# Loading the GLU's gate weights ahead of its value weights, and giving the transposes of the gated product a PSUM bank of their own

## The chip, the core and the metric

The kernel runs on one core of a Trainium2 chip. The metric is the device time of one execution in microseconds (us); three runs of the kernel before were timed and their median counts. Engines are named as in the profile: PE (TensorE matmuls), PEld (TensorE weight loads, which overlap with PE), DVE (VectorE), ACT (ScalarE), POOL (GpSimd) and SP (SyncE, which issues most DMAs). One execution is also profiled, and every number from a trace belongs to that execution.

## The reference: what is computed

One layer of a hybrid encoder on a sequence of 2048 tokens, model width 1024, all in float32. The input is normed and projected into six groups of 512 columns. One group goes through a state-space model, a GELU and a GLU; three more are q, k and v of an 8-head stick-breaking attention; the last two gate these results. Both are joined, projected by W_out and added to the input. Last comes a gated product: a second norm, a projection by W_pg, a sigmoid, and a product with a second, smaller projection of another input p.

```
proj = rmsnorm(x) @ w_in                    # u, g_ssm, q, k, v, g_attn
z    = gelu(S5(u))
val, gate = split(z @ w_glu + b_glu)        # the GLU: w_glu is 512 x 1024
y_ssm = val * sigmoid(gate) * silu(g_ssm)
y_att = stick_breaking(q, k, v) * silu(g_attn)
h    = x + concat(y_ssm, y_att) @ w_out     # the mixed product
out  = h + sigmoid(rmsnorm(h) @ w_pg) * (p @ w_pp)   # the gated product
```

## The kernel before

The work goes through four stages. The first (to about 120 us) projects and prepares the state-space inputs. The second runs the state-space model in eight batches, with the first gate projections. The third is the attention: four passes, each for a pair of heads, over 16 blocks of 128 queries; the passes are staggered by SKEW = 8 steps, so that there are 40 steps (L1215) in which up to two passes are active. In the last ten steps, from glu_at = 30 on, the GLU runs beside the last passes. The fourth stage is phase_out (L1032): eight "mixed" pairs (L945) of 128-token blocks through W_out, then eight "gated" pairs (L988) through W_pg. Both use a seven-product scheme for a 2 x 2 block matrix product (cross_products, L903).

**Precision.** Every float32 operand is split into a rounded part "hi" and a remainder "lo" (split, L511: an ACT copy, then a DVE subtraction), and each product takes three matmuls (mm3, mm3x).

**Weights.** load_w (L473) loads a weight matrix in blocks of 128 x 512 (256 KB). For each block it takes a tile of the ring "w" (16 buffers), a staging buffer "wst" (two buffers at that time), issues the DMA on SP (L486), and splits the block into the tile: ACT copy (L513 by way of L488), DVE subtraction. The DMA of a block can't start until a staging buffer is free, and the copy can't start until the tile's earlier contents are no longer needed.

**GLU.** glu_load (L666) loads the two halves of w_glu, each of four blocks: half 0 makes "val", half 1 makes "gate". It is called once, at the end of step glu_at - 1 (L1243), and loads half 0, then half 1. Of the eight tiles that it takes in the ring, the first four were last used by pass 1 of the attention, the other four by pass 2, whose last projection is in step glu_at - 1. glu_z (L671) loads and splits z: four DMAs "zt" per 512 tokens. glu_unit (L684) computes one 128 x 512 piece of the output: the gate's twelve matmuls into bank "ssm" (tile ps_g2, shown as ps_g in the profile), the value's twelve into bank "acc" (ps_v), then ACT sigmoid, DVE, POOL, and a DMA.

**PSUM.** There are eight banks, named by tags: z0, z1, tr, acc, ssm, o, and w0, w1. bank(name, *tags) (L1120) deals out the given tags in turn for each name. Until step 29 the attention's projections use acc, ssm and tr in turn, later acc and tr only (L44), which leaves ssm to the GLU's gate.

**Gated product.** gated_pair (L988) works on a pair of 128-token blocks, as four tiles h[0] to h[3] of 128 x 512. Each tile is loaded (L995, ring "h" of seven buffers), transposed by four PE transposes into one bank (ps_t, L997 to L999), and copied by ACT to a "yq" tile (L1001, ring of five). cross_products then makes sums and differences of these (POOL, tag "sx", L912), splits them, and runs seven products of twelve matmuls into four accumulators ps[0] to ps[3] (L921): six tags in turn. early and late (L1009, L1014) take the accumulators out: late(k) adds on DVE, takes a sigmoid on ACT (L1020), computes the second weight's product p @ w_pp of six matmuls into ps_p (L1021), multiplies on DVE (L1025), adds h (L1026), and stores. The second weight's product needs nothing but its weights, p and a bank, so it may run early. ps_t and ps_p both take "tr" and "o" in turn.

**Order.** The order of the instructions on each engine isn't the program's. A planner (arrange, L1554; list_schedule, L1446) collects all instructions with their dependencies and durations of its own estimate, simulates the engines forward and backward six times, and keeps the order with the shortest simulated end. Each engine then executes in that order and waits where its next instruction isn't ready. A tile of a tag is opened in the order of the program. The planner picks the most urgent of the instructions that it takes to be ready, and if there is one only, that one.

Of the kernel before, what the change touches and what calls it, by code (L numbers as in the profile page):

```python
# [74 lines left out]
def stt(nc, out, a, s, b, op0, op1):  # L75
    nc.vector.scalar_tensor_tensor(out, a, s, b, op0=op0, op1=op1)  # L76
# [396 lines left out]
def load_w(e, blocks, width, scale, tag="w", pool=None, bufs=None, at=0, act=True, spare=None):  # L473

    nc = e.nc
    out = []
    for c, src in enumerate(blocks, at):
        t = (pool or e.wpool).tile([P, 2, width], F32R, tag=tag, name=f"w_{tag}", **({"bufs": bufs} if bufs else {}))
        hi, lo = t[:, 0], t[:, 1]
        if spare is None or c < STB + STA:  # L480
            raw = e.stage[c % len(e.stage)].tile([P, 512], F32, tag="wst", name="wst")[:, :width]
        else:
            raw = spare.tile([P, L, NCH // 2], F32, tag="uq", name="wst", bufs=4).rearrange("p j c -> p (j c)")[:, :width]
        if c == MARK0 and spare is not None:
            e.mark(0)
        e.wdma(raw.rearrange("p (k c) -> p k c", k=src.shape[1]) if len(src.shape) == 3 and src.shape[0] == P else raw, src)  # L486
        if scale is None:
            split(e, hi, lo, raw)  # L488
        else:
            if act:  # L490
                nc.scalar.activation(hi, raw, AF.Copy, scale=scale[:, c:c + 1])  # L491
            else:
                vs(nc, hi, raw, scale[:, c:c + 1], ALU.mult)
            stt(nc, lo, raw, scale[:, c:c + 1], hi.bitcast(F32), ALU.mult, ALU.subtract)
        out.append(t)
    return out
# [14 lines left out]
def split(e, hi, lo, src):  # L511

    e.nc.scalar.activation(hi, src, AF.Copy)  # L513
    vt(e.nc, lo, src, hi.bitcast(F32), ALU.subtract)
# [148 lines left out]
    return xt  # L663


def glu_load(e):  # L666
    rows = e.w_glu[0].rearrange("(g h) n -> h g n", h=GH)
    return [load_w(e, [rows[4 * c:4 * c + 4, :, 512 * k:512 * k + 512] for c in range(4)], 512, None) for k in range(2)]


def glu_z(e, pool, tb):  # L671
# [231 lines left out]
def cross_products(e, pool, name, q, w, early, late, eng=None):  # L903

    nc = e.nc

    def f(tag, n):
        return pool.tile([P, 512], F32, tag=tag, name=tag, bufs=n)

    def add(a, b, op=ALU.add):  # L910
        t = f("sx", 3)
        (eng or nc.gpsimd).tensor_tensor(t, a, b, op=op)  # L912
        return t

    def product(ps, a, k, first):
        y = pool.tile([P, 2, 4, P], F32R, tag="yr", name="yr", bufs=4)
        split(e, y[:, 0].rearrange("p c t -> p (c t)"), y[:, 1].rearrange("p c t -> p (c t)"), a)
        for c in range(4):
            mm3x(e, ps, (y[:, 0, c], y[:, 1, c]), (w[k][c][:, 0], w[k][c][:, 1]), first and c == 0, c == 3, not first)

    ps = [e.bank(name, "z0", "z1", "acc", "ssm", "w0", "w1") for _ in range(4)]  # L921
    product(ps[0], q[0], 0, True)
    s1 = add(q[2], q[3])
    s2 = add(s1, q[0], ALU.subtract)
    r = f("r", 1)
    nc.scalar.activation(r, ps[0], AF.Copy)
    product(ps[1], s2, 1, True)
    u = f("u", 2)
    vt(nc, u, ps[1], r, ALU.add)
    product(ps[2], s1, 2, True)  # L930
    early(u, ps[2], 0)
    s3 = add(q[0], q[2], ALU.subtract)
    product(ps[3], s3, 3, True)
    early(u, ps[3], 1)
    product(ps[0], q[1], 4, False)
    late(0, ps[0], None)
    late(3, None, None)
    s4 = add(q[1], s2, ALU.subtract)
    product(ps[2], s4, 5, False)
    late(1, ps[2], u)  # L940
    product(ps[3], q[3], 6, False)
    late(2, ps[3], u)
# [45 lines left out]
def gated_pair(e, pool, far, j, rs):  # L988

    nc = e.nc  # L990
    q, h = [], []
    for k in range(4):
        i, m = k // 2, k % 2
        t = far.tile([P, 512], F32, tag="h", name="h", bufs=7)
        nc.sync.dma_start(t, e.h_d[2 * j + i][:, 512 * m:512 * m + 512])  # L995
        h.append(t)
        ps = e.bank("ps_t", "tr", "o")  # L997
        for c in range(4):
            nc.tensor.transpose(ps[:, c * P:(c + 1) * P], t[:, c * P:(c + 1) * P], e.ident)  # L999
        y = pool.tile([P, 512], F32, tag="yq", name="yq", bufs=5)  # L1000
        nc.scalar.activation(y, ps, AF.Copy)  # L1001
        q.append(y)
    pt = far.tile([P, 2, 256], F32, tag="pt", name="pt", bufs=1)
    nc.sync.dma_start(pt, e.p[0, 0].rearrange("(c p) t -> p c t", p=P)[:, :, 256 * j:256 * j + 256])
    pr = far.tile([P, 2, 2, 256], F32R, tag="pr", name="pr", bufs=1)
    split(e, pr[:, 0].rearrange("p c t -> p (c t)"), pr[:, 1].rearrange("p c t -> p (c t)"), pt.rearrange("p c t -> p (c t)"))
    o = [None] * 4

    def early(u, ps, n):  # L1009
        if n == 0:  # L1010
            o[3] = far.tile([P, 512], F32, tag="sg", name="sg", bufs=4)
        vt(nc, o[3], ps, o[3] if n else u, ALU.add)

    def late(k, ps, u):  # L1014
        i, m = k // 2, k % 2
        if o[k] is None:
            o[k] = far.tile([P, 512], F32, tag="sg", name="sg", bufs=4)
            if u is not None:
                vt(nc, o[k], ps, u, ALU.add)
        nc.scalar.activation(o[k], ps if k == 0 else o[k], AF.Sigmoid, scale=rs[:, i:i + 1])  # L1020
        pp = e.bank("ps_p", "tr", "o")  # L1021
        ts = slice(i * P, i * P + P)
        for c in range(2):
            mm3x(e, pp, (pr[:, 0, c, ts], pr[:, 1, c, ts]), (e.wp[m][c][:, 0], e.wp[m][c][:, 1]), c == 0, c == 1)
        vt(nc, o[k], pp, o[k], ALU.mult)  # L1025
        (nc.vector if j == NT // 2 - 1 else nc.gpsimd).tensor_tensor(o[k], o[k], h[k], op=ALU.add)  # L1026
        nc.sync.dma_start(e.out[0, (2 * j + i) * P:(2 * j + i + 1) * P, 512 * m:512 * m + 512], o[k])

    cross_products(e, pool, "ps_g", q, e.wg, early, late)


# [13 lines left out]
def hybrid_block_kernel(ctx: ExitStack, tc: tile.TileContext, x, xt, small, p, w_in, ssm_w_glu, w_out, w_ple_gate,  # L1045
                        w_ple_proj, out, rows, pools, dbg=None):
    nc = tc.nc
    e = Env()
# [59 lines left out]
    def pool(stack, name, bufs=1, space=None, side=None):  # L1108
        kw = {} if space is None else {"space": space}
        if side:  # L1110
            kw["side"] = side
        pools.append(stack.enter_context(tc.tile_pool(name=name, bufs=bufs, reuse_waits="tile", **kw)))
        return pools[-1]
# [58 lines left out]
    with e.later():  # L1172
        wgate = load_w(e, row_blocks(e.w_in[0], NC8, 512), 512, e.gmix)
# [19 lines left out]
    t = 0  # L1193
# [27 lines left out]
    glu_at = steps - 10  # L1221
    for t in range(steps):
        e.z_banks, e.q_banks, e.o_banks = BANKS[2 if t < SKEW - 2 else t >= glu_at]
        for hp in range(NHP):
            if 0 <= t - SKEW * hp < NT:
                attn_block(e, ap, A[hp], t - SKEW * hp)
        if t == glu_at:
            over.close()
            gl = pool(over, "glu")
        for hp in range(NHP):  # L1230
            i = t - SKEW * hp
            if 0 <= i + 2 < NT and i + 2 >= (AHEAD if hp == 0 else 0):
                attn_proj(e, ap1, A[hp], i + 2, xg[:, i % 2] if hp == 0 and i < AHEAD else None)
            if i == -WE and hp:
                attn_w(e, A[hp], 0, 4, **(dict(pool=wx, bufs=4) if hp == 2 else {}))
            if i == -3 and hp:
                attn_w(e, A[hp], 4, NC8)
        if t == AHEAD - 1:
            left.close()
            e.xp = pool(ctx, "xp")  # L1240
            kv2 = pool(left, "kv2")
            wx = pool(over, "wx")
        if t == glu_at - 1:  # L1243
            wglu = glu_load(e)
        if t >= glu_at:
            for k in glu_units[t - glu_at]:
                if k % 4 == 0:
                    zr = glu_z(e, gl, k // 4)
                glu_unit(e, old, (6, 7) if t >= glu_at + 2 else (6,), wglu, zr, k // 4, k % 4)
            c = t - glu_at - 2  # L1250
            if c >= 0:
                cross_sums(e, old, *((w_out[0], e.so_d, None) if c < 4 else (w_ple_gate[0], e.sg_d, e.gple)), c % 4)
        if t == steps - 3:
            e.wo = [cross_weights(e, e.w_out[0], e.so_d, None, p) for p in range(2)]
            wo4 = cross_weights(e, e.w_out[0], e.so_d, None, 4, pool=Halves(e))
# [358 lines left out]
```

## Time and profile before

| | |
|---|---|
| timed runs | 1490.81, 1491.39, 1494.24 us; median 1491.39 |
| the profiled execution's own time | 1490.92 us |
| its span in the trace | 1489.2 us |
| its mean granted TensorE clock | 0.995 |
| first GLU gate matmul, first GLU value matmul | 863.6 us, 879.4 us after the span's start |
| transposes of the gated product (128 of them) | from 1254.8 to 1459.1 us |
| last second-weight matmul | 1484.1 us |

In lines of the timeline and of the groups, the columns are: start, duration (or count), engine, line of the kernel, operation, output <- inputs, shapes; in brackets the idle time of the engine just before and what ended it. Lines of waits give who waited, for whom, the total in us, how many times, and the longest. Lines of windows give the stretch, its length, the busy time of each engine with its instructions, the granted clock of PE (1.00 is full speed), and the DMA engines' share and rate. L65, L76 and L513 are lines of helpers that serve many places, so there the tile names tell which one is meant.

### The profile page before, as it was taken

To read this page: it belongs to the slowest core of one execution; us is meant where nothing else is said; L and a number is where in the kernel's file an instruction comes from. 1 tells how busy PE (TensorE), PEld (TensorE's weight loads), DVE (VectorE), ACT (ScalarE), POOL (GpSimd) and SP (SyncE) were. 2 spreads that over 40 slices of the span, in tenths; PEclk is the share of its full clock that TensorE was granted. 3 is DMA by queue.
4 is the path that set the end of the run, shared out by engine and by line. 5 is a ranking of instruction groups with operands and counts; after the bars stand their busy time and mean duration, and the time that the engine had idled before them with its cause. 6 is when DMAs were issued, how large, how long until landed. Compare 5 with 4: busy or idle time off the path is not lost.

```text
span 1489.2 us, 33570 instructions
## 1 busy us (share of the span) xinstructions
PE 1444.9 (97%) x13068; PEld 1220.6 (82%) x13068; DVE 1012.0 (68%) x1814; ACT 812.1 (55%) x1764; POOL 469.2 (32%) x512
## 2 busy tenths in 40 slices
PE   5999999999999999999999999999999999999998
PEld 5999989988888888887788877787777888777776
DVE  8943877976567876777766766657777557744544
ACT  5654545565456765566655655566654436533333
POOL 3221354412221111211122114544234555434332
PEclk9999999999999999999999999999999999999999
DMA  8876746645332523334333445766477546423221
GB/s 292 296 267 231 227 135 206 194 152 169 126 131 99 180 99 101 126 120 141 97 125 126 125 131 183 234 223 187 131 243 243 170 156 196 151 76 107 72 67 60
DMA packets 178909, 238.21 MB, mean 160 GB/s; under 512 B 65744, under 2 KB 121024, under 8 KB 167616
## 3 DMA queue, kind: packets, MB, share of 16 engines
q1 hardware_dynamic: 176368, 227.49, 47.2%
q0 software_dynamic: 2384, 8.59, 2.0%
q8 instruction: 103, 1.69, 0.5%
q14 instruction: 54, 0.44, 0.1%
HBM read 166.94 MB, written 64.90 MB: 156 GB/s over the span
## 4 chain that ended last, share of the span: by engine, by line
PE 77%; DVE 9%; DMA 4%; issue 4%; ACT 3%; POOL 2%; SPq 1%; DVEq 0%; POOLq 0%; ACTq 0%
PE ps_q L745 20%; PE ps_o L843 7%; PE ps_z L812 6%; PE ps_wt L526 4%; PE ps_g L707 4%; PE ps_g L709 4%; PE ps_g L708 3%; PE ps_h L709 3%; PE ps_h L707 3%; PE ps_h L708 3%; DMA wst<-in_ssm_w_glu_dram 2%; PE ps_u L541 1%; PE ps_u L543 1%; PE ps_u L542 1%; PE ps_sg L541 1%
## 5 line engine op out<-in xcount | busy, mean ns | idle before, releaser
L821 DVE TENSOR_TENSOR_SCAN px<-px,ps_z 128x512 f32<-128x512 f32 (+3 forms) x320 | 339.4, 1085 | 102.6 <-ACT px L816 64.5
L745 PE MATMUL ps_q<-w_w,xt 64*128 64x512 f32 x2784 | 372.5, 398 | 1.6 <-DVE old L76 0.9
L745 PEld LDWEIGHTS ps_q<-w_w,xt 64*128 64x128 f32 x2784 | 269.1, 185 | 41.1 <-DVE old L76 1.5
L816 ACT ACTIVATE px<-ps_z 128x512 f32<-128x512 f32 (+3 forms) x320 | 159.5, 534 | 82.5 <-PE ps_z L812 80.8
L835 ACT ACTIVATE ws<-ps_wt 128x512 f32<-128x512 f32 (+3 forms) x320 | 160.3, 537 | 71.8 <-PE ps_wt L526 67.4
L812 PE MATMUL ps_z<-k,q 64*128 64x512 f32 (+3 forms) x960 | 138.0, 381 | 2.1 <-DVE px L821 1.1
L843 PE MATMUL ps_o<-ws,v 128*64 128x128 f32 x2176 | 136.9, 278 | 0.0
L843 PEld LDWEIGHTS ps_o<-ws,v 128*64 128x64 f32 x2176 | 118.6, 138 | 17.0 <-issue 13.7
L507 POOL TENSOR_TENSOR rs_qk<-rs_qk,mhalf 128x4 f32<-128x4 f32 x64 | 67.2, 1050 | 186.5 <-DVE rs_qk L72 183.9
L526 PEld LDWEIGHTS ps_wt<-ident,px 64*128 64x128 f32 x2176 | 94.5, 139 | 29.1 <-ACT ws L835 8.0
L526 PE MATMUL ps_wt<-ident,px 64*128 64x64 f32 x2176 | 100.5, 224 | 5.7 <-ACT ws L835 5.0
L812 PEld LDWEIGHTS ps_z<-k,q 64*128 64x128 f32 x960 | 86.9, 186 | 21.8 <-issue 5.4
L819 POOL TENSOR_SCALAR_AFFINE_SELECT px<-px 128x128 f32<-128x128 f32 x128 | 40.5, 326 | 175.7 <-ACT px L816 167.5
L756 POOL TENSOR_TENSOR v<-qn,v 128x128 f32<-128x128 f32 x64 | 30.9, 483 | 167.6 <-DMA v<-qn 147.8
L541 PE MATMUL ps_u<-xt,w_w 128*128 128x256 f32 x256 | 74.3, 292 | 8.1 <-ACT w_w L491 6.8
L543 PE MATMUL ps_u<-xt,w_w 128*128 128x256 f32 x256 | 73.2, 292 | 2.9 <-DVE w_w L76 2.9
L542 PE MATMUL ps_u<-xt,w_w 128*128 128x256 f32 x256 | 73.8, 289 | 0.5 <-DVE xt L65 0.5
L1026 POOL TENSOR_TENSOR sg<-sg,h 128x512 f32<-128x512 f32 x28 | 39.3, 1412 | 99.7 <-DVE sg L65 90.7
L65 DVE TENSOR_TENSOR yr<-sx,yr 128x512 fp32r<-128x512 f32 x64 | 49.2, 790 | 31.1 <-ACT yr L513 30.2
L65 DVE TENSOR_TENSOR qn<-ps_q,part 128x512 f32<-128x512 f32 x54 | 36.8, 682 | 44.2 <-ACT part L751 40.9
L513 ACT ACTIVATE yr<-sx 128x512 fp32r<-128x512 f32 x64 | 39.3, 629 | 50.2 <-POOL sx L912 17.6
L541 PEld LDWEIGHTS ps_u<-xt,w_w 128*128 128x128 f32 x256 | 50.3, 197 | 8.9 <-ACT w_w L491 7.0
(438 smaller groups left out, 3464.0 us busy)
## 6 DMA issues: line engine op xcount, KB each, us to landing
xt<-hn SPq DMA_DIRECT2D x58, 1024.0 KB
hn<-xt SPq DMA_DIRECT2D x16, 1024.0 KB
h<-h SPq DMA_DIRECT2D x64, 256.0 KB
wst<-in_w_in_dram SPq DMA_DIRECT2D x48, 256.0 KB
xg<-hn SPq DMA_DIRECT2D x12, 1024.0 KB
out_dram<-sg SPq DMA_DIRECT2D x32, 256.0 KB
x<-in_x_dram SPq DMA_DIRECT2D x14, 512.0 KB
h<-in_x_dram SPq DMA_DIRECT2D x28, 256.0 KB
```

The costliest lines, as they stand in the source:

```text
L526: e.nc.tensor.transpose(ps[h][:, 64 * k:64 * k + 64], v[r], e.ident[r, r])
L541: mm(out, wh, xh, start=first, stop=False)
L542: mm(out, wh, xl, start=False, stop=False)
L707: mm(out, xh, wh, start=first, stop=False, skip_group_check=more)
L708: mm(out, xh, wl, start=False, stop=False, skip_group_check=more)
L709: mm(out, xl, wh, start=False, stop=last, skip_group_check=more)
L745: nc.tensor.matmul(o, xt[r, a, c], A.w[c][r, b], start=c + s == 0, stop=c == NC8 - 1 and s == 2)
L812: nc.tensor.matmul(z[:, :n], q[half[h], a], A.k[ch][half[h], b, :n], start=s == 0, stop=s == 2)
L816: nc.scalar.activation(px[:, :n], z[:, :n], AF.Sigmoid, scale=-(HD ** -0.5))
L821: nc.vector.tensor_tensor_scan(rv, rv, z[:, :n][:, ::-1], initial=1.0 if carry[h] is None else carry[h], op0=ALU.mult, op1=ALU.bypass)
L835: nc.scalar.activation(dst, ps, AF.Copy, bias=1.0, scale=-1.0)
L843: nc.tensor.matmul(po[half[h], :P], A.v[sb][:, h], w[:, h, b], start=sb == i, stop=sb == 0)
```

## The change

glu_load now loads one half. The gate half is loaded at the end of step glu_at - 4, the value half at the end of step glu_at - 1. Nothing else is allocated from the ring of weight tiles or from the staging buffers between the two places, so the gate half gets the four tiles that pass 1 had, and the value half the four that pass 2 had. In the gated product the accumulators take five tags in turn (without w1), the second weight's products take o and w1 in turn, and the transposes take tr only. The mixed product keeps its six tags. The planner's code is the same; it plans the whole program anew.

```diff
-def glu_load(e):
+def glu_load(e, k):
     rows = e.w_glu[0].rearrange("(g h) n -> h g n", h=GH)
-    return [load_w(e, [rows[4 * c:4 * c + 4, :, 512 * k:512 * k + 512] for c in range(4)], 512, None) for k in range(2)]
+    return load_w(e, [rows[4 * c:4 * c + 4, :, 512 * k:512 * k + 512] for c in range(4)], 512, None)
...
-    ps = [e.bank(name, "z0", "z1", "acc", "ssm", "w0", "w1") for _ in range(4)]
+    ps = [e.bank(name, "z0", "z1", "acc", "ssm", "w0", *(("w1",) if name == "ps_h" else ())) for _ in range(4)]
...
-        ps = e.bank("ps_t", "tr", "o")
+        ps = e.bank("ps_t", "tr")
...
-        pp = e.bank("ps_p", "tr", "o")
+        pp = e.bank("ps_p", "o", "w1")
...
+        if t == glu_at - 4:
+            wgate = glu_load(e, 1)
         if t == glu_at - 1:
-            wglu = glu_load(e)
+            wglu = [glu_load(e, 0), wgate]
```

## The prediction

> **What bounds the kernel now.** I read the page's busy times first, then the windows by stage, then PE's waits, and last the timelines of the two places that the change touches.
>
> ```profile
> span 1489.2 us, 33570 instructions
> PE 1444.9 (97%) x13068; PEld 1220.6 (82%) x13068; DVE 1012.0 (68%) x1814; ACT 812.1 (55%) x1764; POOL 469.2 (32%) x512
> ```
>
> PE is the bound: 1489.2 - 1444.9 leaves 44.3 us of the span without a matmul. A change that removes no matmul can win only from these 44.3 us, and from time in which matmuls run slowly. The windows show where they lie.
>
> ```profile
> core 0: us, PE busy (x) PEld busy (x) DVE busy (x) ACT busy (x) POOL busy (x), PEclk, DMA share, GB/s
> 670.00:700.00 30.00, 27.60 (x342) 22.70 (x342) 20.88 (x37) 18.14 (x44) 4.73 (x8) 0.94 0.48 146
> 846.00:870.00 24.00, 19.89 (x246) 16.14 (x244) 17.71 (x28) 15.86 (x34) 3.38 (x6) 0.93 0.71 169
> 1255.00:1485.00 230.00, 226.17 (x1016) 177.97 (x1014) 123.67 (x164) 93.37 (x158) 85.37 (x62) 1.00 0.30 95
> ```
>
> The second row is the start of the GLU: 24 - 19.89 = 4.1 us idle, at a mean clock of 0.93. The third is the gated product: 230 - 226.17 = 3.8 us idle in 230 us. The first row holds the early loads of GLU weights. PE's waits name what ended the idle time, and the weight loads' wait of the last stage stands beside them.
>
> ```profile
> PE ps_g L541 <- DVE qn L65: 3.2, 1, 3.2
> PE ps_t L999 <- DVE sg L65: 2.8, 6, 0.5
> ...
> PEld ps_t L999 <- DVE sg L65: 4.5, 7, 0.7
> ```
>
> So the GLU has one wait of 3.2 us before its first gate matmul, and the gated product has six of 0.47 us before transposes. These are the two targets.
>
> **The GLU weights.** Now the value half is loaded first. Its four blocks and two of the gate half's come early, and the gate half's last two come when pass 2 has given up its weights:
>
> ```profile
> 672.91 1.34 SPq L486 DMA_DIRECT2D wst<-in_ssm_w_glu_dram  x2
> 685.25 7.93 SPq L486 DMA_DIRECT2D wst<-in_ssm_w_glu_dram  x3
> 702.54 0.61 SPq L486 DMA_DIRECT2D wst<-in_ssm_w_glu_dram  x1
> 846.37 0.64 SPq L486 DMA_DIRECT2D wst<-in_ssm_w_glu_dram  x1
> 850.41 5.08 SPq L486 DMA_DIRECT2D wst<-in_ssm_w_glu_dram  x1
> ```
>
> The edit gives the four tiles that are free at 672 to the gate half and the others to the value half. The ring of weight tiles and the two staging buffers are walked in the same sequence, as nothing else is allocated from them between the two places; so the eight DMAs, the eight ACT copies and the eight DVE subtractions are the same in number and size, and I expect them at nearly the same places. On SP the four gate loads then stand among the attention's xt, v and ya transfers of 672 to 703, where four value loads stand now; the late ones stand behind zt transfers, as two gate loads do now. POOL's queue has none of them. Their cost as work is nothing new: what hid them hides them. What can change is the stall. These lines of ACT, DVE and PE tell what it is:
>
> ```profile
> 856.34 1.09 ACT L835 ACTIVATE ws<-ps_wt 128x512 f32<-128x512 f32 x2 [0.53 <-PE ps_wt L526]
> 861.68 0.63 ACT L513 ACTIVATE w_w<-wst 128x512 fp32r<-128x512 f32 x1 [4.26 <-DMA wst<-in_ssm_w_glu_dram]
> 862.22 0.58 ACT L751 ACTIVATE part<-ps_q 128x512 f32<-128x512 f32 x1
> 862.83 0.69 DVE L65 TENSOR_TENSOR qn<-ps_q,part 128x512 f32<-128x512 f32 x1 [4.78 <-ACT part L751]
> 863.58 0.79 PE L541 MATMUL ps_g<-zr,w_w 128*128 128x512 f32 x1 [3.19 <-DVE qn L65]
> ```
>
> PE doesn't wait for the gate's weights. It waits for bank "ssm", which still holds a projection; its eviction (L751, then DVE) stands on ACT behind the copy of the gate half's last block, and that copy waits 4.26 us for its DMA. The DMA was issued at 850.41 and its copy starts at 861.68: 11.3 us. So the block at fault is "the last of eight", whichever half it is in. After the edit the last of eight is a value block, which is needed later:
>
> ```profile
> L541 PE MATMUL ps_v<-zr,w_w x64: 388/389/499, 879.4 to 1086.7; 128*128 128x512 f32 x64
> ```
>
> The first value matmul is at 879.4, 879.4 - 863.6 = 15.8 us behind the first gate matmul. That lowers the copy's urgency in the planner. But ACT idles in this stretch (0.53 us just before), and the planner gives an idle engine whatever its own estimate says is ready; it expects the DMA long before 861.68, or the copy would not stand ahead of L751. So the cost of this edit lies between nothing and the whole stall. The stall's price has a second part, the clock:
>
> ```profile
> 692.00:694.00 2.00, 1.88 (x24) 1.82 (x26) 2.00 (x4) 1.83 (x6) 0.00 (x0) 0.71 0.19 66
> 694.00:696.00 2.00, 2.00 (x16) 1.47 (x14) 1.86 (x4) 1.63 (x5) 0.00 (x0) 0.50 0.57 119
> ...
> 862.00:864.00 2.00, 0.42 (x1) 0.43 (x2) 1.17 (x2) 2.00 (x5) 0.00 (x0) 0.87 0.91 153
> 864.00:866.00 2.00, 2.00 (x13) 1.14 (x14) 2.00 (x3) 2.00 (x5) 0.00 (x0) 0.50 0.93 290
> 866.00:868.00 2.00, 2.00 (x32) 2.00 (x30) 1.05 (x4) 0.59 (x3) 0.80 (x1) 0.77 1.07 319
> ```
>
> From 862 to 868 the granted clock fell short by 2 x (0.13 + 0.50 + 0.23) = 1.7 us of PE time. The whole stall is 3.2 + 1.7 = 4.9 us. The two rows at 692 show the same after a wait of 1.7 us only:
>
> ```profile
> 692.12 0.34 PE L526 MATMUL ps_tq<-ident,qn 64*128 64x64 f32 x4 [1.68 <-ACT g L791]
> ```
>
> The Trainium skill, "TensorE: Matmul & The Clock Gate", Part 1 (What's actually happening), says that the clock halves after an idle window of about 3.4 us; by that a wait of 3.2 us might cost only itself. This trace differs: 1.68 us of waiting were followed by 0.50, so I keep the 1.7 us. By that rule alone the stall would be worth 3.2.
>
> I take 0 for this edit as the likeliest, since the cause is the last block's lateness and the edit leaves a last block; the other end is -4.9. Below nothing it cannot well go by itself, as every gate block now comes no later than before.
>
> **The banks of the gated product.** No operation is added or removed. Now transposes and the second weight's products share "tr" and "o" in turn. This is one boundary between pairs of blocks:
>
> ```profile
> 1313.93 0.39 PE L709 MATMUL ps_g<-w_wc,yr 128*128 128x512 f32 x1
> 1314.16 0.39 PE L707 MATMUL ps_p<-w_wp,pr 128*128 128x512 f32 x1
> ...
> 1315.53 0.60 PE L999 MATMUL ps_t<-ident,h 128*128 128x128 f32 x4
> 1316.59 1.09 PE L999 MATMUL ps_t<-ident,h 128*128 128x128 f32 x8 [0.47 <-DVE sg L65]
> 1317.56 0.50 PE L707 MATMUL ps_g<-w_w,yr 128*128 128x512 f32 x1
> ...
> 1318.13 0.60 PE L999 MATMUL ps_t<-ident,h 128*128 128x128 f32 x4
> ...
> 1343.67 0.60 PE L999 MATMUL ps_t<-ident,h 128*128 128x128 f32 x4
> 1344.74 1.09 PE L999 MATMUL ps_t<-ident,h 128*128 128x128 f32 x8 [0.46 <-DVE sg L65]
> ```
>
> The last product ends (1313.93), a second-weight product fills 1.37 us, then come the transposes. The second group needs "o", which holds the last second-weight product of the pair before until DVE has multiplied by it:
>
> ```profile
> 1315.84 0.69 DVE L65 TENSOR_TENSOR sg<-ps_p,sg 128x512 f32<-128x512 f32 x1 [0.79 <-ACT sg L1020]
> ```
>
> 1315.84 + 0.69 is 1316.53, and the transpose starts at 1316.59. After the change no transpose waits for such a bank, and the first group may run during the last product, as its copy target (a fifth "yq" buffer) is free. I expect all six waits to go. That is 2.8 us by PE's own row, and up to 4.5 by the weight loads' row, in which the pipeline's loss is fuller. Between them I take 3.5.
>
> What could eat it: a group must now wait for the copy of the group before.
>
> ```profile
> 1316.26 0.58 ACT L1001 ACTIVATE yq<-ps_t 128x512 f32<-128x512 f32 x1
> ```
>
> A group that starts at 1315.53 has its bank free at 1316.26 + 0.58 = 1316.84, 1.3 us later, while PE needs about 0.4 us for the four (1318.13 to the next matmul). So each of the three later groups of a pair needs 0.9 us of other matmuls ahead of it. These exist: two products of the second weight (6 x 0.23 = 1.4 us each) before and two after, and the first product (12 x 0.23 = 2.8 us). If that cover is not used, it costs 0.9 us each.
>
> Next late is the fourth transpose: its input's load needs a buffer that the pair before gives up, and behind it come two POOL subtractions and sums before the second product.
>
> ```profile
> 1314.16 0.42 SPq L995 DMA_DIRECT2D h<-h  x1
> ...
> 1319.51 1.29 POOL L912 TENSOR_TENSOR sx<-yq 128x512 f32<-128x512 f32 x1 [1.23 <-ACT yq L1001]
> 1320.88 1.30 POOL L912 TENSOR_TENSOR sx<-sx,yq 128x512 f32<-128x512 f32 x1
> ```
>
> POOL's two take 1.3 us each and start with the fourth group. They are why I count no more than 4.5: PE can't reach the second product much sooner. Five banks instead of six for accumulators cost nothing by my reading: a pair opens four; the next pair's first product finds the fifth free, its second needs the bank of the accumulator that is evicted earliest, its fourth the one evicted before the last product. The second weight's two banks serve four products per pair as now, without transposes between.
>
> **The sum.** The profiled execution took 1490.92 us, 1.7 over its span; 1490.92 - 3.5 - 0 = 1487.4. It lay 0.5 under the median of 1491.39, so against medians I say 1487.9. A measurement of this kernel can tell about 0.3% from no change, which is 4.5 us: the forecast is within it.
>
> **The rivals.** (1) The GLU's stall goes as well: with the value half less urgent, the planner puts L751 ahead of the late copy. For it speaks the 15.8 us above; against it that ACT had idle time there. It gives 1487.9 - 4.9 = 1483.0, faster by 0.56%. (2) The change does not do what it says: the whole order is planned again, the 0.47 us come back as waits for the single transpose bank or for the fourth input, and the GLU stays. That is about 1491.4, no change. For it speaks how close the fourth group already is to its load. (3) Slower: the single transpose bank serialises PE. Of 8 x 3 = 24 later groups, each that is not covered costs 0.9 us; it is over 0.3% slower once the uncovered ones exceed (4.5 + 3.5) / 0.9 = 9. With 14 of 24 it is 14 x 0.9 - 3.5 = 9.1 us, 1500.5. For it speaks that PE keeps its planned order; against it the fillers named above. The Trainium skill, "Perfetto Trace Analysis", Matmuls, says that independent matmul groups should rotate through PSUM banks so that one's evacuation overlaps the next group's matmuls; the change stops doing so for transposes, and by that rule rival 3 would be the outcome. No row of this trace shows a single bank for transposes in this stage.
>
> **How the numbers follow.** Forecast 0.40, rival 1 0.33, rival 2 0.14, rival 3 0.13. Faster by over 0.3%: rival 1 and the forecast's lower end (4.5 at the boundaries and some of the stall), 0.08, together 0.41. Slower: 0.13. Within: 0.46. The range goes from rival 1 with the fuller boundary gain and a little of the new order's own luck (1483.0 - 1.0 - 0.5 = 1481.5) to a rival 3 of few uncovered groups (1494.0); the forecast's own range is 1485 to 1490.
>
> **What would show it.** Right: PE's wait of ps_t for DVE sg (2.8) gone, the window 1255:1485 with under 1 us idle, first transposes of a pair ahead of the end of the last product; ACT's copy of a late GLU block still waiting some 4 us near 860. Rival 1: that copy behind L751, and no clock of 0.50 there. Rival 3: a row "ps_t <- ACT yq" of over 5 us among PE's waits. The prediction is wrong if the time moves elsewhere: a new wait before 846, where the change has no operation but the whole order is planned anew, or a longer tail after 1485.

## The result, and the profile after

| | before | changed |
|---|---|---|
| median, first lot (4 runs each) | 1491.83 us | 1483.87 us |
| ratio, 95% interval | | 0.9946 (0.9928 to 0.9963) |
| median, run again (17 and 6 runs) | 1493.35 us | 1482.74 us |
| ratio, 95% interval | | 0.9930 (0.9917 to 0.9942) |
| span of the profiled execution | 1489.2 us | 1481.9 us |

The changed kernel is faster by 0.54% in the first lot and by 0.70% in the second: 8 to 10.6 us. The predicted 1487.9 us was 4 us too high; the time lies below the forecast's own 1485 to 1490 and inside the whole range, at the place of rival 1 (1483.0). The page's first lines show that the matmuls are the same work.

```profile
span 1481.9 us, 33584 instructions
PE 1443.8 (97%) x13068; PEld 1223.0 (83%) x13068; DVE 1011.5 (68%) x1814; ACT 810.8 (55%) x1764; POOL 473.7 (32%) x512
```

PE is as busy as before to 1.1 us. The time without a matmul went from 44.3 to 1481.9 - 1443.8 = 38.1 us. The windows say where. First two stretches of the kernel before that the prediction did not quote:

```profile
950.00:1000.00 50.00, 49.08 (x518) 40.32 (x515) 30.28 (x46) 29.33 (x65) 24.11 (x26) 1.00 0.73 241
1060.00:1105.00 45.00, 43.51 (x438) 34.92 (x438) 33.50 (x41) 27.46 (x54) 11.22 (x14) 1.00 0.56 172
```

And the changed kernel's windows, with the start of the GLU first and the gated product last (the changed kernel is ahead by then, so the last stretch is cut at 1478):

```profile
846.00:870.00 24.00, 23.07 (x290) 18.54 (x288) 21.47 (x33) 19.19 (x40) 5.56 (x7) 1.00 0.74 161
950.00:1000.00 50.00, 50.00 (x501) 41.19 (x497) 30.91 (x43) 29.21 (x64) 24.50 (x27) 1.00 0.70 231
1060.00:1105.00 45.00, 44.52 (x441) 35.42 (x437) 33.18 (x44) 27.39 (x52) 11.83 (x15) 1.00 0.58 185
1255.00:1478.00 223.00, 219.00 (x991) 172.74 (x989) 118.57 (x157) 89.89 (x151) 84.54 (x61) 1.00 0.29 93
```

At the start of the GLU the idle time fell from 4.11 to 0.93 us and the clock from 862 to 868 is full (it was worth 1.7). In the two later stretches it fell by another 0.92 and 1.01 us. Together that is 3.2 + 1.7 + 1.9 = 6.8 us. The span fell by 7.3 us, which seems to leave 0.5 us for the banks. But the changed kernel's profiled execution was already 1.2 us behind at its first attention projection (L745, at 316.3 us and 315.1 before), where the orders are still the same. From the first matmul of the mixed product to the end it took 386.9 us (1095.0 to 1481.9), and the kernel before 388.8 (1100.4 to 1489.2): the fourth stage gave 1.9 us, and 6.8 + 1.9 - 1.2 = 7.5. The last row surprises: 223 - 219.00 = 4.0 us idle, 0.8 of it behind the last matmul. The other 3.2 are about as many as before (3.8 in 230 us, 0.5 of it behind the last matmul). The timelines explain both. At the GLU (SP and ACT):

```profile
847.62 0.64 SPq L486 DMA_DIRECT2D wst<-in_ssm_w_glu_dram  x1
...
858.28 1.90 SPq L486 DMA_DIRECT2D wst<-in_ssm_w_glu_dram  x1
...
860.77 0.63 ACT L751 ACTIVATE part<-ps_q 128x512 f32<-128x512 f32 x1
...
866.21 0.63 ACT L513 ACTIVATE w_w<-wst 128x512 fp32r<-128x512 f32 x1 [1.24 <-DMA wst<-in_ssm_w_glu_dram]
```

The last of the eight blocks is issued even later than before (at 858.28; it was 850.41) and its copy again waits for the DMA (1.24 us). But the eviction L751 now stands ahead of that copy on ACT: 860.77 and 866.21, where it was 862.22 behind 861.68. PE has no wait for it. PE's order is another one here, too: the first gate matmul comes at 872.9 us (863.6 before) and the first value matmul at 877.0 (879.4 before).

One boundary of the gated product (PE, ACT, POOL), with the first pair's new wait ahead of it:

```profile
1263.80 0.50 PE L707 MATMUL ps_g<-w_w,yr 128*128 128x512 f32 x1 [1.20 <-ACT yr L513]
...
1339.61 0.60 PE L999 MATMUL ps_t<-ident,h 128*128 128x128 f32 x4
1339.96 0.48 PE L707 MATMUL ps_g<-w_w,yr 128*128 128x512 f32 x1
1340.34 0.58 ACT L1001 ACTIVATE yq<-ps_t 128x512 f32<-128x512 f32 x1
...
1341.20 0.60 PE L999 MATMUL ps_t<-ident,h 128*128 128x128 f32 x4
...
1342.58 0.60 PE L999 MATMUL ps_t<-ident,h 128*128 128x128 f32 x4
...
1344.02 1.29 POOL L912 TENSOR_TENSOR sx<-yq 128x512 f32<-128x512 f32 x1 [1.67 <-ACT yq L1001]
...
1345.40 1.29 POOL L912 TENSOR_TENSOR sx<-sx,yq 128x512 f32<-128x512 f32 x1
...
1346.49 0.60 PE L999 MATMUL ps_t<-ident,h 128*128 128x128 f32 x4
...
1346.72 1.15 ACT L513 ACTIVATE yr<-sx 128x512 fp32r<-128x512 f32 x2 [2.20 <-POOL sx L912]
...
1347.40 0.50 PE L707 MATMUL ps_g<-w_w,yr 128*128 128x512 f32 x1 [0.32 <-ACT yr L513]
```

No transpose waits on PE any more: the groups stand singly among other matmuls. The three groups from 1339.61 on are the second to fourth of their pair. Its first group ran in the pair before, at the place where 1346.49 stands here for the next pair: the first product starts at 1339.96, before ACT copies the group of 1339.61 (1340.34), and at the last boundary only three groups are left (from 1449.6 on). In place of the 0.47 us stands a wait of 0.32 us, at the second product, for ACT's split of POOL's second sum, which ends at 1345.40 + 1.29. And the first pair has a new wait of 1.20 us. The kernel's waits show the exchange: PE's and the weight loads' lines.

```profile
PE ps_g L707 <- ACT yr L513: 3.1, 7, 1.2
...
PEld ps_t L999 <- ACT yq L1001: 1.8, 9, 0.3
```

The pairs are shorter all the same. From the first transposes of one boundary to those of the next it was 1343.67 to 1371.79, and is now 1339.61 to 1367.21: 28.12 and 27.60 us. These windows are cut there, before and then after:

```profile
1343.67:1371.79 28.12, 27.66 (x125) 21.77 (x124) 13.19 (x17) 10.26 (x18) 10.95 (x8) 1.00 0.26 84
```

```profile
1339.61:1367.21 27.60, 27.28 (x125) 21.67 (x124) 12.65 (x17) 10.26 (x18) 10.98 (x8) 1.00 0.28 86
```

Of the 0.52 us, 0.14 is idle time and 0.38 is busy time of the same matmuls. The ends of matmuls are modelled, and a matmul after a break is shown longer (0.50 us at 1347.40, 0.39 or 0.40 within a row of them), so a wait that breaks the row seems to cost more than its own bracket. The weight loads' 4.5 us against PE's 2.8 us had pointed the same way.

### The profile page after: what moved, and what is told of

It is laid out like the page before. It is cut to its first block, busy times and chain, and to the rows that moved or that the text cites. A ratio compares the mean times of both kernels' runs of the same rounds, so it can differ in the third digit from the quotient of the medians.

```text
span 1481.9 us, 33584 instructions
## 1 busy us (share of the span) xinstructions
PE 1443.8 (97%) x13068; PEld 1223.0 (83%) x13068; DVE 1011.5 (68%) x1814; ACT 810.8 (55%) x1764; POOL 473.7 (32%) x512
## 4 chain that ended last, share of the span: by engine, by line
PE 79%; DVE 9%; ACT 3%; issue 3%; DMA 3%; POOL 2%; SPq 0%; POOLq 0%; ACTq 0%; DVEq 0%
PE ps_q L745 21%; PE ps_o L843 7%; PE ps_z L812 6%; PE ps_wt L526 4%; PE ps_g L707 4%; PE ps_h L709 4%; PE ps_h L708 4%; PE ps_h L707 4%; PE ps_g L709 3%; PE ps_g L708 3%; PE ps_u L541 1%; PE ps_u L543 1%; PE ps_u L542 1%; POOL sx L912 1%; PE ps_sg L541 1%
## 5 line engine op out<-in xcount | busy, mean ns | idle before, releaser
L745 PE MATMUL ps_q<-w_w,xt 64*128 64x512 f32 x2784 | 375.9, 399 | 0.7 <-ACT part L751 0.5
L745 PEld LDWEIGHTS ps_q<-w_w,xt 64*128 64x128 f32 x2784 | 271.0, 186 | 39.0 <-DVE qn L65 1.3
L835 ACT ACTIVATE ws<-ps_wt 128x512 f32<-128x512 f32 (+3 forms) x320 | 161.1, 538 | 76.9 <-PE ps_wt L526 70.7
L541 PE MATMUL ps_u<-xt,w_w 128*128 128x256 f32 x256 | 75.5, 296 | 8.1 <-ACT w_w L491 6.9
L543 PE MATMUL ps_u<-xt,w_w 128*128 128x256 f32 x256 | 74.1, 295 | 2.0 <-DVE w_w L76 2.0
L542 PE MATMUL ps_u<-xt,w_w 128*128 128x256 f32 x256 | 74.9, 294 | 0.5 <-DVE xt L65 0.5
L513 ACT ACTIVATE yr<-yq 128x512 fp32r<-128x512 f32 x48 | 30.3, 631 | 55.5 <-PE ps_h L709 24.2
```

The costliest lines, as they stand in the source:

```text
L541: mm(out, wh, xh, start=first, stop=False)
L542: mm(out, wh, xl, start=False, stop=False)
L745: nc.tensor.matmul(o, xt[r, a, c], A.w[c][r, b], start=c + s == 0, stop=c == NC8 - 1 and s == 2)
L835: nc.scalar.activation(dst, ps, AF.Copy, bias=1.0, scale=-1.0)
```

## The experiments

All kernels compute the whole of the reference. Each was timed in five rounds against the kernel before on the same chip, and the differences below are between medians there. The ratios with their intervals go by means, so the two can differ a little.

**The two parts alone.** The gate part is glu_load(e, k) with its two calls; the bank part is the three edits of bank tags. One line of each:

```diff
+            wgate = glu_load(e, 1)          # only in the gate part
...
-        pp = e.bank("ps_p", "tr", "o")      # only in the bank part
+        pp = e.bank("ps_p", "o", "w1")
```

> The kernel before with the GLU part of the change alone; the gated product keeps its banks. Theory A (the stall at the GLU's start, a late weight block whose copy stands on ACT ahead of a projection's eviction, goes when that block belongs to the value half): the gain of the stretch from 846 to 1105 us, about 6 us, so 0.4% faster, and no clock of 0.50 near 864. Theory B (the banks made the gain, the GLU part is neutral): within 1 us of the kernel before, with the 3.2 us wait still there.

> The kernel before with the gated product's banks alone; both GLU halves load as before. Theory A: 2 us faster (some 0.5 us at each of seven boundaries, less about 1.8 us lost in the first gated pair), and the wait of 3.2 us at the GLU stays. Theory B: 6 us or more faster.

The gate part took 1485.47 us beside 1493.27: -7.8 us, ratio 0.9944 (0.9929 to 0.9959). The bank part took 1490.78: -2.5 us, ratio 0.9983 (0.9973 to 0.9994). The two add up to -10.3, about what the whole change gave in the second lot. So the part that the forecast put at nothing carries most of the gain. In the bank part the wait of the GLU stays, and the first pair's new wait is larger, 2.8 us (PE's waits of that kernel):

```profile
PE ps_g L707 <- ACT yr L513: 4.3, 6, 2.8
PE ps_g L541 <- DVE qn L65: 2.9, 1, 2.9
```

**One copy moved, in each direction.** Loads, banks and the order of every other instruction stay; only the ACT copy of the last of the eight GLU blocks is moved in ACT's finished order. In the kernel before it goes 7 places later, behind L751; in the gate-part kernel 9 places earlier, ahead of L751.

```diff
+    at = line.index(copy)      # line: ACT's planned order
+    line.remove(copy)
+    line.insert(at + 7, copy)  # at - 9 in the other kernel
```

> The kernel before in the order it had, with one instruction moved: on ACT, the copy of the GLU's last weight block stands seven places later, behind the eviction L751. Loads, halves, banks and the order on all other engines are as before. If the stall is this one copy standing in the queue ahead of the eviction while its DMA is on the way (theory A): 3.2 us of wait and 1.7 us of lost clock go, 4 to 5.5 us faster than before, ratio near 0.997. If the stall is the block's lateness itself or the order of the halves (theory C): no change, because the block lands at the same time.

> The kernel with the GLU part of the change alone in the order it had, with one instruction moved: on ACT, the copy of the last weight block (a value block) stands nine places earlier, ahead of the eviction L751. Theory A: ACT then stands until the block lands near 865 us, about 6 us, and the stall is back: 4 to 8 us slower than the GLU part alone, so about as slow as the kernel before or slower. Theory C (gate half first is what counts): no change against the GLU part alone, 0.994 of before.

Later: 1488.72 us beside 1493.67, -4.9 us, ratio 0.9972 (0.9963 to 0.9981). Earlier: 1493.21, +7.7 us beside the gate part's 1485.47 and as slow as before, ratio 0.9997 (0.9989 to 1.0006). (The two lots' kernels before differ by 0.4 us.) The first kernel's window and ACT lines:

```profile
846.00:870.00 24.00, 22.01 (x280) 17.87 (x277) 20.88 (x32) 18.56 (x40) 3.56 (x7) 1.00 0.74 162
```

```profile
859.50 0.60 ACT L751 ACTIVATE part<-ps_q 128x512 f32<-128x512 f32 x1 [0.41 <-PE ps_q L745]
...
865.31 0.62 ACT L513 ACTIVATE w_w<-wst 128x512 fp32r<-128x512 f32 x1
```

And the second kernel's timeline of ACT and PE:

```profile
866.58 0.63 ACT L513 ACTIVATE w_w<-wst 128x512 fp32r<-128x512 f32 x1 [6.03 <-DMA wst<-in_ssm_w_glu_dram]
...
867.59 0.59 ACT L751 ACTIVATE part<-ps_q 128x512 f32<-128x512 f32 x1
...
868.23 2.47 PE L745 MATMUL ps_q<-w_w,xt 64*128 64x512 f32 x6 [5.19 <-ACT part L751]
```

With the gate's weights loaded first, and all eight loads in the gate part's order, the old stall is back as soon as the copy stands ahead of the eviction, and longer: 5.2 us. This shows the cause of the stall. It isn't which half comes first, but what ACT does while the last block is under way. What waits on PE differs: the gate's first matmul before, and here a projection (L745) that takes the bank which the eviction frees. The first experiment gives the price of the stall in the kernel before, 4.9 us, which is the prediction's 3.2 + 1.7.

**Telling the planner.** If the place of the copy comes from the planner's estimate of the load, a corrected estimate should move it. Nothing but the estimate is changed:

```diff
-            done[k] = link + 2.0
+            done[k] = link + 2.0 + (7.0 if k in tail else 0.0)   # tail: the last two GLU blocks
```

> The kernel before, with one thing changed in the planner alone: it is told that the last two blocks of the GLU's weights land 7 us later than it took them to; loads, banks and program are those of before. Theory A (the stall at 863 comes from the planner's wrong estimate of that load, by which it puts the copy ahead of the eviction that the gate's bank waits for): the eviction L751 stands ahead of the late copy, the wait of 3.2 us and the low clock at 864 are gone, 4 to 6 us faster, about 1488. Rival (the gain of the changed kernel lies in which half comes last, not in where the copy stands): the wait moves to the gate's last block, whose matmuls come first, and the time is within 1.5 us of before. As the planner orders the stretch from some 690 us on anew, up to 2 us of either sign can come from elsewhere; the row of the window 846:870 decides.

1491.40 us beside 1493.35, ratio 0.9990 (0.9979 to 1.0001): 2 us or nothing, not the 4 to 6 expected. Its window and its ACT and PE lines:

```profile
846.00:870.00 24.00, 19.28 (x252) 16.92 (x250) 16.87 (x27) 16.09 (x33) 4.17 (x5) 0.90 0.66 137
```

```profile
859.47 0.60 ACT L751 ACTIVATE part<-ps_q 128x512 f32<-128x512 f32 x1
...
865.91 1.07 ACT L513 ACTIVATE zr<-zt 128x512 fp32r<-128x512 f32 x1 [5.57 <-DMA zt<-z]
...
867.31 1.12 PE L526 MATMUL ps_wt<-ident,px 64*128 64x64 f32 x16 [4.49 <-ACT ws L835]
```

The first half came as expected: the eviction now stands ahead, at 859.47, and the wait for qn is gone. But the planner put another copy there, that of a zt block whose load was issued behind the same transfers and is as late; the eviction L835 stood behind it, and PE waited 4.49 us. The window is no better than before (4.7 us idle, clock 0.90). The estimate does set the place of the copy. The zt block, whose estimate was not corrected, kept ACT waiting for 5.57 us, so one correction seems to have moved the mistake to the next load. That the changed kernel has no such copy in a bad place is thus an outcome of its new plan, not of a rule in it.

**Making the late blocks early.** Here the gate's last two blocks are loaded near 719 into key tiles that are idle then, in the kernel before.

```diff
+        if held is not None and c >= 2:
+            raw = held[:, c - 2]
...
+            wglu = glu_load(e, old(6))
```

> The kernel before, value half first as before, but the last two blocks of the gate half are loaded into an idle tile of the old keys near 710 us and not into the two staging buffers, so that no block of GLU weights arrives after 846 us. If the stall is the late DMA in ACT's queue (theory A): as much faster as the GLU part of the change, 5 to 6 us, without any swap of the halves. If it is the order of the halves that counts, because the gate is used first (theory C): no change, as the gate half still comes second and is still split after pass 2 gave up its tiles.

It missed: 1497.66 us, 4.4 us slower, ratio 1.0025 (1.0012 to 1.0037). The stall at 863 is gone, but two other stretches are worse:

```profile
700.00:745.00 45.00, 40.31 (x508) 32.32 (x506) 29.95 (x46) 25.39 (x56) 8.40 (x16) 1.00 0.37 108
...
846.00:870.00 24.00, 23.06 (x277) 19.02 (x274) 21.47 (x32) 19.98 (x43) 4.17 (x6) 1.00 0.79 186
...
950.00:1000.00 50.00, 47.23 (x474) 37.51 (x472) 26.23 (x39) 25.22 (x55) 24.13 (x26) 0.93 0.64 215
```

From 700 to 745 the idle time is 4.7 us (1.35 before), with the two added loads ahead of xt and v on SP; from 950 to 1000 it is 2.8 us (0.92), and the clock falls. PE's order is that of before up to about 739 us and a new one from there on, so this kernel can't say what an early load is worth. Nor is it shown that the added loads in SP's queue cost this time: PE's waits of 1.39 and 1.26 us ahead of 739 end with DVE's px and not with a load.

**Where the second weight's products find their banks.** GLU as before, transposes on tr, the second weight's products on o alone, six banks for the accumulators:

```diff
-        ps = e.bank("ps_t", "tr", "o")
+        ps = e.bank("ps_t", "tr")
...
-        pp = e.bank("ps_p", "tr", "o")
+        pp = e.bank("ps_p", "o")
```

> The kernel before with transposes on bank tr alone and the second weight's products on bank o alone; the accumulators keep six banks and the GLU loads as before. If the gain at the pair boundaries comes from parting transposes and products (theory F): 28.1 us for a pair become 27.6 as in the banks-only kernel, 1 to 3 us faster than before. If the second bank for the products is what matters (rival G): the products wait for each other's DVE multiplication, a pair stays at 28.1 us or longer, no change or slower.

1497.38 us, 3.7 us slower than before, ratio 1.0041 (1.0026 to 1.0056). Its profiled execution was the slowest of the seven (1503.95 us) and lost 7 us ahead of the mixed product, where PE's order is that of before, so only the pairs are read. A pair takes 28.25 us (between the same transposes of two pairs, at 1355.11 and 1383.36), and PE waits for ACT's yr at eight places, 3.0 us at one and (8.7 - 3.0) / 7 = 0.8 at the others:

```profile
PE ps_g L707 <- ACT yr L513: 8.7, 8, 3.0
```

So taking the transposes out of the shared banks is not enough: with it alone a pair is no shorter than before (28.1), as the rival expectation had it. It takes the second bank for the products as well (27.6), and that is worth more than the sixth bank of the accumulators, which the change gives up for it. How the single bank lengthens the pair isn't shown, as PE's named waits are for ACT and not for that bank. No kernel gave the products a further bank and left the transposes in the shared ones, so what parting them is worth by itself stays open.

**The new waits of the gated product.** Three kernels ask after them: the changed kernel with the gated sums on DVE instead of POOL (run twice), with two banks for the transposes of the first pair alone, and with both.

```diff
-    cross_products(e, pool, "ps_g", q, e.wg, early, late)
+    cross_products(e, pool, "ps_g", q, e.wg, early, late, nc.vector)   # sums on DVE
...
-        ps = e.bank("ps_t", "tr")
+        ps = e.bank("ps_t", "tr") if j else e.bank("ps_t0", "tr", "o")  # first pair
```

> The changed kernel with the gated product's sums and differences on DVE in place of POOL. Theory D (at each boundary PE now waits for the chain fourth transpose, two POOL operations of 1.3 us, split): the 0.32 us waits before the second product go, 7 x 0.32 = 2.2 us faster than the changed kernel. Rival E (the wait is set by the load or by the single transpose bank): no change, or slower by the DVE time that is added, 32 x 0.7 us beside other work.

> The changed kernel, but the first gated pair's transposes take tr and o in turn, as before. Theory H (the new wait of 1.2 us before the first pair's second product comes from its transposes being served one after the other from one bank, so that the sums of the fourth come late): the wait goes, 1 to 2 us faster than the changed kernel. Rival I (it comes from the new place of the first pair in the order, with POOL and ACT still busy for the mixed pair): no change.

> The changed kernel with the gated sums on DVE instead of POOL, once more, now beside the changed kernel. Theory D (POOL's two sums of 1.29 us between the fourth transposes and the second product are what costs 0.3 us at a boundary): 2 us faster than the changed kernel, about 0.9985 of its time. Rival (another wait of the same size has taken their place, the pair lasts 27.6 us with either): the same as the changed kernel within 1 us, and the earlier lower ratio was the chip's.

> The changed kernel with the gated sums on DVE, and with two banks, tr and o, for the transposes of the first gated pair alone. If the loss at the first gated pair (1.2 us of waiting for ACT's yr in the changed kernel) comes from the single bank or from POOL's sums: 1 to 1.5 us faster than the changed kernel with DVE sums alone. If it comes from the splits of the last weights, which fill ACT and DVE there: the same as that kernel within 1 us.

> The changed kernel once more, as the common yardstick for the three kernels beside it. Both theories: 1484 to 1487 us, a ratio of 0.993 to 0.996 to the kernel before, with 27.6 us from one gated pair to the next, and 0.3 us at each boundary for ps_g behind ACT's yr.

Sums on DVE: 1481.91 us beside 1493.27, ratio 0.9923 (0.9906 to 0.9939), then 1482.29 beside 1493.35, 0.9926 (0.9912 to 0.9941); the changed kernel itself had 1482.74, 0.9930 (0.9917 to 0.9942), in that second lot, somewhat less than the 1484 to 1487 us expected. The expected 2 us are not there. POOL's wait has gone, and one of the same size stands in its place (PE's waits of the kernel with DVE sums):

```profile
PE ps_p L707 <- ACT pr L513: 1.9, 6, 0.3
```

A pair takes 27.57 us instead of 27.60, although all four of its transpose groups stand at the boundary in this kernel (1338.70 to 1343.15). So a first group that runs early isn't what makes the pairs short. Two banks for the first pair: 1483.13 us beside 1493.67, ratio 0.9933 (0.9921 to 0.9945), and its first wait is still 1.0 us. So the single bank didn't cause the loss at the first pair. With both edits the 1.2 us wait is gone from the list, and the time is 1482.30 us, the same as with DVE sums alone:

```profile
PE ps_p L707 <- ACT pr L513: 1.9, 6, 0.3
...
PE ps_p L707 <- ACT yq L1001: 0.7, 1, 0.7
```

Fewer waits in the list again bought nothing. What sets the time at the first pair is left open: ACT and DVE also split the last weights there, which fits, but no kernel moved these splits away. No version clearly beats the changed kernel; the intervals of all four overlap.

## Why the prediction was right and wrong

**What bounds the kernel** held. PE's work stayed, and the gain came from idle time and from the low clock.

**The GLU: the failed step** is "I take 0 for this edit as the likeliest, since the cause is the last block's lateness and the edit leaves a last block". The diagnosis before it was right, and its price too: moving that one copy is worth 4.9 us (by the interval 2.8 to 5.5), where 3.2 + 1.7 had said the same. The edit does leave a last block, and a later one. But the lateness costs only what stands behind the copy on ACT. The prediction had named both the urgency (15.8 us) and the planner's estimate, and gave more weight to the second; in the new plan the copy came behind L751. The telling run is the one with the copy put back: +7.7 us. That the lower urgency put the copy there isn't shown: in the new plan the first value matmul follows the first gate matmul after 877.0 - 872.9 = 4.1 us, not 15.8.

The size was off as well: the other end was -4.9, and the part alone gave -7.8. Its plan also has less idle time between 950 and 1105, where the GLU's matmuls stand in another order: 0.5 us in the two later windows with the gate part alone, 2.4 before, and still 2.1 in the kernel where only the copy was moved. That is 1.9 us. The prediction had no term for it: it priced the edit at the place of the stall alone, although it had said that the whole order is planned anew. The remaining 1 us is less than the intervals can tell.

**The banks.** All six waits went, as forecast, and the pairs became 0.52 us shorter; seven such steps are 3.6 us, the forecast's 3.5. The cover for the single transpose bank was there in all pairs: PE has no wait of ps_t for yq, the weight loads 1.8 us in nine waits. The term that was left out is the first pair, where a new wait of 1.2 us (2.8 in the bank part alone) takes back a third or more; measured alone the part gave 2.5, and the fourth stage in the traces 1.9. Of the signs that were named for this part, the first transposes of a pair do run ahead of the end of the last product, and by more than was thought: one group at 1346.49 belongs to the pair whose other three start at 1367.21. "Under 1 us idle" failed, for the reason that the prediction gave as its cap: POOL's two sums behind the fourth group. That they were next late was right; that removing them would gain nothing, because ACT's copy of pr is as late, came out only in the run. "Five banks instead of six for accumulators cost nothing" stands: no wait for an accumulator's bank appears.

**The rivals.** Rival 1 came, with its two signs as written: that copy behind L751, full clock from 862 to 868. That its 1483.0 was hit so closely is partly luck, as its two terms missed in opposite directions: 7.8 instead of 4.9 us for the GLU, 2.5 instead of 3.5 for the banks. Rival 2's first half (waits that come back under other names) was true of the boundaries, without eating the gain. Rival 3 didn't come. Nor did the rule beside it: the Trainium skill, "Perfetto Trace Analysis", Matmuls, wants independent groups to rotate through banks so that evacuation overlaps. Here the four transposes of a group take 0.6 us and have over 0.9 us of other matmuls behind them, so one bank is enough; for the second weight's products, which come two and two in a row, the times go the way of the rule (28.25 us a pair with one bank, 27.60 with two), though no wait for that bank is named.

## What to carry to other kernels

A late DMA costs what is queued behind the instruction that waits for it, so look at the consumer's engine and its order before the transfer: one copy seven places later was worth 4.9 us here, and nine places earlier 7.7. Where a planner orders by estimates, a change of urgency can move such a copy by chance, and correcting one estimate can hand the same place to the next late load; price the edit with both outcomes. When a wait is removed, count what is late next at the same place and in the first and last round of the loop, and measure a shorter list of waits by the time of a round (28.12 against 27.60 us), not by the sum of the waits.

## What the runs showed of the hardware

The clock's answer to the same wait differs from run to run. Up to about 818 us PE's order is the same in these kernels; PE waits for ACT's g near 692 us in each. In the kernel before, 1.68 us of it were followed by 0.50 of the clock. In the changed kernel the wait was longer and the clock stayed full; the dip came at the next wait (PE lines and windows of the changed kernel):

```profile
693.18 0.34 PE L526 MATMUL ps_tq<-ident,qn 64*128 64x64 f32 x4 [1.96 <-ACT g L791]
...
718.28 0.97 PE L812 MATMUL ps_z<-k,q 64*128 64x512 f32 x5 [1.70 <-DVE px L821]
```

```profile
694.00:696.00 2.00, 2.00 (x28) 1.72 (x26) 1.87 (x4) 1.84 (x6) 0.00 (x0) 1.00 0.44 55
...
720.00:722.00 2.00, 2.00 (x17) 1.41 (x15) 1.86 (x3) 1.85 (x5) 0.00 (x0) 0.50 0.35 131
```

In the kernel with the copy moved later, 2.27 us at the same place brought 0.50 again. The Trainium skill, "TensorE: Matmul & The Clock Gate", Part 1 (What's actually happening), says that the window in which activity is watched runs freely, so that a change of clock depends on where in it the matmuls fall. These runs agree with that, but not with the whole idle window of 3.4 us that the page asks for: 1.68 and 1.70 us sufficed. Each of the three dips (two near 694, one near 720) cost about 1.7 us of PE time by the rows of the clock, so two profiled spans that differ by that much need their clock rows read before anything else.
